# Value products with the values stationary, and three attention groups mixed feature by feature

## The chip, the core and the metric

The kernel runs on one core of a Trainium2 chip. The metric is device time in microseconds (us) of one execution. The kernel before took 1386.01 us, the median of three runs (1385.64, 1386.01 and 1386.95).

The engines are named as in the profile: PE multiplies matrices and writes PSUM, DVE and ACT do elementwise work, POOL does little here beside issuing transfers to its own software queue, and SP issues most transfers to a hardware queue. Each engine takes its instructions in program order, so an instruction that waits holds up everything behind it on that engine.

## The reference, cut to what matters

The program is one encoder layer for 1024 tokens of width 1024, all in float32. Its mixer A is a mixture of three dilated attention groups, four heads of 64 features each; the groups look at keys with a stride of 1, 4 and 16 tokens. For each token and head slot the three outputs are combined with weights that come from the softmax denominators:

```python
    s = jnp.einsum('brnqhd,brnkhd->brnhqk', qb, kw).astype(jnp.float32) * (dh ** -0.5) + bias
    s = jnp.where(mask[:, :, None], s, NEG_INF)
    m = jnp.max(s, axis=-1, keepdims=True)
    e = jnp.exp(s - m)
    den = jnp.sum(e, axis=-1, keepdims=True)
    o = jnp.einsum('brnhqk,brnkhd->brnhqd', e, vw) / den
    lse = (m + jnp.log(den))[..., 0]
...
        mix_w = jax.nn.softmax(jnp.stack(lses, axis=0), axis=0)
        y_attn = jnp.sum(mix_w[..., None] * jnp.stack(outs, axis=0), axis=0)
...
        merged = (jax.nn.sigmoid(gate_a) * (y_attn @ w_attn_branch[l])
                  + jax.nn.sigmoid(gate_g) * (y_gla @ w_gla_branch[l]))
```

The rest of the layer (the input projection, the gated linear attention, the output projection, two layer norms and the MLP) is left as it is by the change.

## The kernel before, in words

The large products are done by `mm3` (L97): each float32 operand is split into a high and a low part, and three matmuls (L101, L102, L103) take the place of one. Everything here concerns the stretch from about 300 us to 600 us, in which the input projection's remaining blocks run on PE and the attention is woven into them.

**Steps.** The projection blocks form a list `steps`; each step is one product of 12 matmuls over 512 columns with its evacuation from PSUM on DVE or ACT (L642 is the addition that evacuates most). A step's weights are prepared three steps ahead. The dictionary `units` hangs other work on a step's number: the attention's visits, and the gating of the other mixer.

**Visits.** `att(g, t)` makes the parts of one tile: group g, 128 queries t. There are 24 tiles, and `visit(i)` (L931) runs for neighbouring tiles, in this order, `load` of tile i+1 (POOL fetches queries and keys, L770), `values` of tile i-2, `scores` of tile i (POOL fetches the values, then PE computes the scores at L803, two heads at a time in the two halves of the array's rows, DVE adds the bias at L809 and ACT exponentiates at L814), `turned` of tile i-1 (PE transposes the exponentials at L830, and they are copied to `et`), then `mix` and `mixed`. The 27 visits are spread evenly over the steps. The tiles go by group: all eight of group 2, then of group 1, then of group 0.

**Value products** (L844). For each block of keys and each head, PE holds the transposed exponentials (keys x 128 queries) and streams the values (keys x 64 features) through; the result has a query per partition and 4 x 64 features in `avp`. Group 2 has one block of keys per tile, the other groups have two. A float32 product is two passes of the array, so the profile counts 320 matmuls for 160 products.

**Mixing.** Groups 2 and 1 write numerators and denominators of a tile as rows of 264 values to DRAM (`rows`, L857 and L859). A tile of group 0 reads the two other groups' rows back (L821), works out the weights (`weigh`, L878 to L884), multiplies and adds on DVE (`blend`, L887 to L898), transposes the result back to features on PE (L872), and writes it to `yadr` (L874): once per tile, eight times in all.

**Handing over.** After the attention, `branches` reads `yadr` back with SP (L963, tile `pre`), and ACT and DVE split it into high and low parts (`ya`, L148 and L149): four pieces, two feature halves by two halves of the tokens. `merge_a` (L1020) multiplies them by the branch weights, `merge_g` does the same for the other mixer's `yg`. That is the next work PE has after the last step.

**What sets the order.** The program is recorded in the order of the code, and a scheduler then orders each engine's instructions by its own time model. What is fixed is the data's dependences and the buffers.

Of the kernel before, what the change touches and what calls it, by code (L numbers as in the profile page):

```python
# [7 lines left out]
F32 = mybir.dt.float32  # L8
# [3 lines left out]
AF = mybir.ActivationFunctionType  # L12
# [5 lines left out]
S = 1024  # L18
# [53 lines left out]
def build(tc, io):  # L72
# [40 lines left out]
    rows = dr.tile([2, S, 264], F32, name="rows")  # L113
# [463 lines left out]
    px = cx.tile([128, 2, 512], F32R, name="px")  # L577
    wt = [[wp.tile([128, 2, 512], d, tag=t, bufs=n, name="p" + t) for _ in range(n)]
# [168 lines left out]
    sm_t, f_t = ring(ap_, [128, 8], F32, 3, "sm"), ring(ap_, [128, 5, 4], F32, 2, "f")  # L747
    st_t, R_t = ring(ap_, [128, 264], F32, 2, "st"), ring(ap_, [128, 3, 264], F32, 2, "R")
# [3 lines left out]
    yat = ap_.tile([128, 2, 128], F32, name="yat")  # L752
# [9 lines left out]
    def att(g, t):  # L762
# [54 lines left out]
        def turned():  # L817
            if g == 0:
                b["R"] = R_t()
                for i in range(2):  # L820
                    G.dma_start(b["R"][:, 1 + i], rows[i, t * 128:t * 128 + 128])  # L821
# [17 lines left out]
        def values():  # L839
            nb = len(b["blks"])  # L840

            def part(j, h):
                lo, hi, vv, p0 = b["blks"][j]
                return T.matmul(av[:, h * 64:h * 64 + 64], b["et"][h % 2][p0:p0 + vv.shape[0], h // 2, j],  # L844
                                vv[:, h * 64:h * 64 + 64], start=j == h == 0, stop=j == nb - 1,
                                skip_group_check=True)
# [6 lines left out]
            st = b["R"][:, 0] if g == 0 else st_t()  # L853
            V.tensor_copy(st[:, 0:256], av)
            V.tensor_copy(st[:, 256:264], b["sm"])
            if g == 1:
                G.dma_start(rows[0].rearrange("(u j c) w -> c u j w", u=2, c=4)[t // 2, t % 2], st)  # L857
            elif g == 2:
                G.dma_start(rows[1].rearrange("(j r) w -> r j w", r=8)[t], st)  # L859
            else:  # L860
                b["f"] = weigh(b["R"])

        def mix():
            if g == 0:
                b["o"] = o = st_t()[:, 0:256]
                blend(b["R"], b["f"], o)

        def mixed():
            if g == 0:
                tp = tr_t()  # L870
                for pr in range(2):
                    T.transpose(tp[:, pr, 0:128], b["o"][:, pr * 128:pr * 128 + 128], ident)  # L872
# [931 lines left out]
```

## Time and profile before

| what | us |
|---|---|
| median of three runs | 1386.01 |
| span of the profiled execution | 1382.5 |
| PE busy in it | 1373.9 (99%) |
| DVE busy | 1010.4 (73%) |
| ACT busy | 630.6 (46%) |
| POOL busy | 99.3 (7%) |

The page gives no time for the profiled execution other than its span, 1382.5 us from the first to the last instruction; the three runs are timed around the whole execution, and their median is 3.5 us longer. A change in the span is therefore carried over to the median as it is.

A row of the trace that begins with two numbers gives the start in us from the span's start and the length in us, then the engine, the line, the operation, the tiles (written <- read), the array's rows*columns in use, the shape and the count. A row with slashes gives the shortest, median and longest duration of a group in ns.

### The profile page before, as it was taken

To read this page: it belongs to the slowest core of one execution; us is meant where nothing else is said; L and a number is where in the kernel's file an instruction comes from. 1 tells how busy PE (TensorE), PEld (TensorE's weight loads), DVE (VectorE), ACT (ScalarE), POOL (GpSimd) and SP (SyncE) were. 2 spreads that over 40 slices of the span, in tenths; PEclk is the share of its full clock that TensorE was granted. 3 is DMA by queue.
4 is the path that set the end of the run, shared out by engine and by line. 5 is a ranking of instruction groups with operands and counts; after the bars stand their busy time and mean duration, and the time that the engine had idled before them with its cause. 6 is when DMAs were issued, how large, how long until landed. Compare 5 with 4: busy or idle time off the path is not lost.

```text
span 1382.5 us, 19028 instructions
## 1 busy us (share of the span) xinstructions
PE 1373.9 (99%) x6837; PEld 1152.6 (83%) x6837; DVE 1010.4 (73%) x1748; ACT 630.6 (46%) x1207; POOL 99.3 (7%) x153
## 2 busy tenths in 40 slices
PE   9999999999999999999999999999999999999998
PEld 7989998888888888888888788888888888888886
DVE  6377768776665678567757777877767897786988
ACT  5356645334434344455316655555456433333333
POOL 0000100022322232000001000000000000000002
PEclk9999999999999999999999999999999999999999
DMA  7262326765554443465934465656654965445313
GB/s 256 62 204 74 120 72 219 205 198 156 172 163 136 133 148 125 153 226 190 342 121 177 168 233 191 215 204 213 224 200 150 373 210 167 152 130 161 105 31 122
DMA packets 105907, 238.57 MB, mean 173 GB/s; under 512 B 20101, under 2 KB 28805, under 8 KB 105812
## 3 DMA queue, kind: packets, MB, share of 16 engines
q1 hardware_dynamic: 99220, 218.47, 47.4%
q0 software_dynamic: 6304, 18.49, 4.4%
q8 instruction: 54, 0.88, 0.3%
q10 hardware_dynamic: 288, 0.39, 0.1%
q14 instruction: 41, 0.34, 0.1%
HBM read 160.67 MB, written 77.68 MB: 172 GB/s over the span
## 4 chain that ended last, share of the span: by engine, by line
PE 96%; DVE 2%; ACT 1%; issue 0%; DMA 0%; SPq 0%; ACTq 0%; DVEq 0%
PE ps L101 18%; PE ps L103 18%; PE ps L102 18%; PE mm L101 10%; PE mm L102 10%; PE mm L103 10%; PE avp L844 3%; PE sc L803 2%; PE tr L830 2%; PE ps L1192 0%; PE sc L406 0%; PE tr L376 0%; DVE L L341 0%; PE sc L101 0%; PE sc L103 0%; PE sc L102 0%
## 5 line engine op out<-in xcount | busy, mean ns | idle before, releaser
L1176 ACT CAST T<-hp 128x1024 fp32r<-128x1024 f32 x36 | 37.8, 1050 | 110.3 <-PE ps L102 70.6
L102 PE MATMUL mm<-wlo,x 128*128 128x272 f32 (+1 forms) x240 | 74.5, 310 | 0.7 <-DVE wlo L94 0.7
L101 PE MATMUL mm<-whi,x 128*128 128x272 f32 (+1 forms) x240 | 75.0, 313 | 0.0
L103 PE MATMUL mm<-whi,x 128*128 128x272 f32 (+1 forms) x240 | 74.7, 311 | 0.0
L814 ACT ACTIVATE e<-e,sm 128x256 f32<-128x256 f32 (+2 forms) x96 | 43.4, 453 | 51.7 <-DVE sm L809 51.7
L102 PE MATMUL ps<-B,B 128*128 128x512 f32 x160 | 62.4, 390 | 0.0
L103 PE MATMUL ps<-B,B 128*128 128x512 f32 x160 | 62.3, 389 | 0.0
L101 PE MATMUL ps<-B,B 128*128 128x512 f32 x160 | 61.0, 391 | 0.5 <-ACT B L1176 0.5
L103 PE MATMUL ps<-B,T 128*128 128x512 f32 x144 | 56.2, 390 | 0.0
L101 PE MATMUL ps<-B,T 128*128 128x512 f32 x144 | 56.2, 390 | 0.0
L103 PE MATMUL ps<-T,T 128*128 128x512 f32 x144 | 56.1, 390 | 0.0
L101 PE MATMUL ps<-T,T 128*128 128x512 f32 x144 | 56.0, 389 | 0.0
L102 PE MATMUL ps<-T,T 128*128 128x512 f32 x144 | 56.0, 389 | 0.0
L102 PE MATMUL ps<-B,T 128*128 128x512 f32 x144 | 56.0, 389 | 0.0
L1177 DVE TENSOR_TENSOR T<-hp,T 128x1024 fp32r<-128x1024 f32 x36 | 43.9, 1220 | 15.3 <-ACT T L1176 15.2
L1577 DVE TENSOR_TENSOR acc<-ps,acc 128x512 f32<-128x512 f32 x68 | 45.5, 684 | 12.9 <-PE ps L103 12.2
L642 DVE TENSOR_TENSOR cr<-cu,mm 128x512 f32<-128x512 f32 x44 | 35.1, 799 | 23.7 <-PE mm L103 23.5
L1682 POOL TENSOR_TENSOR mv<-mv,mhalf 128x1 f32<-128x1 f32 x8 | 7.1, 882 | 611.4 <-DVE mv L1681 609.9
L101 PE MATMUL mm<-x,pwlo 128*128 128x512 f32 x128 | 51.0, 398 | 0.0
L101 PE MATMUL ps<-T,fraw 128*128 128x512 f32 x128 | 50.0, 394 | 0.3 <-ACT T L1176 0.3
L102 PE MATMUL ps<-T,fraw 128*128 128x512 f32 x128 | 50.1, 392 | 0.0
L103 PE MATMUL ps<-T,fraw 128*128 128x512 f32 x128 | 50.1, 392 | 0.0
(497 smaller groups left out, 4227.3 us busy)
## 6 DMA issues: line engine op xcount, KB each, us to landing
hdr<-c SPq DMA_DIRECT2D x112, 256.0 KB, 2.3
hp<-hdr SPq DMA_DIRECT2D x56, 512.0 KB, 3.6
spill<-cr SPq DMA_DIRECT2D x64, 256.0 KB, 2.8
praw<-in_wfm SPq DMA_DIRECT2D x16, 512.0 KB, 5.0
pwhi<-in_wfm SPq DMA_DIRECT2D x16, 512.0 KB, 4.5
gate<-spill SPq DMA_DIRECT2D x32, 256.0 KB, 3.4
wa<-in_w SPq DMA_DIRECT2D x16, 512.0 KB, 4.7
wb<-in_w SPq DMA_DIRECT2D x16, 512.0 KB, 6.3
```

Of the source, the lines that this page charges most:

```text
L101: T.matmul(ps, lh, rh, start=first and i == 0, stop=False, skip_group_check=more)
L102: T.matmul(ps, lh, rl, start=False, stop=False, skip_group_check=more)
L103: issued["pe"] = T.matmul(ps, ll, rh, start=False, stop=last and i == n - 1, skip_group_check=more)
L642: issued["add"] = V.tensor_tensor(o, a, b, op=OP.add)
L803: mm = T.matmul(sps[i][:, pr, 0:w], q[ps_, pr], k[ps_, pr, 0:w], start=True, stop=True)
L814: issued["exp"] = A.activation(e, e, AF.Exp, bias=sm[:, h:h + 1], scale=-1.0, accum_out=sm[:, 4 + h:5 + h])
L830: T.transpose(tp[0:hi - lo, pr, j], b["e"][i][:, pr, lo:hi], ident)
L844: return T.matmul(av[:, h * 64:h * 64 + 64], b["et"][h % 2][p0:p0 + vv.shape[0], h // 2, j], vv[:, h * 64:h * 64 + 64], start=j == h == 0, ...
L1176: A.copy(o[:, 0], src)
L1177: V.tensor_tensor(o[:, 1], src, o[:, 0].bitcast(F32), op=OP.subtract)
L1577: V.tensor_tensor(m, p, m, op=OP.add)
L1682: G.tensor_tensor(mv[:, 3:4], mv[:, 2:3], mhalf[:, 0:1], op=OP.pow)
```

## The change

Three things are done at once.

1. *Value products.* The values are now the operand that PE holds (keys x 64 features) and the transposed exponentials are streamed through (128 queries). Heads 0 and 2 go to the first 64 columns of the array and heads 1 and 3 to the last 64, so the result `avp` has a feature per partition and a query per column.
2. *Mixing.* All three groups write numerators, feature by feature, to `numdr`, and the maxima and denominators to `smdr`. For each 256 tokens (four times, `mixing(n)`, each in eight pieces hung on eight successive steps) the small values are fetched, the weights are worked out on DVE and ACT, transposed on PE (12 rows) and written to `fdr`. Then, for each half of the features, POOL reads back the numerators of the three groups (`mn`, two buffers) and, spread over 64 partitions, the weights (`mw`, three buffers); DVE multiplies and adds, and POOL writes the half to `yadr`. The transposes of the mixed result are gone.
3. *Order.* Tiles of group 1 and group 0 alternate by halves of the sequence, four and four, so that the first 256 tokens can be mixed at visit 15. There are 26 visits, spread up to three steps before the place where they ended. The pieces of `ya` are read last, after all of `yg`, and by halves of the tokens.

```diff
+    mn_t, mw_t = ring(cx, [128, 256], F32, 2, "mn"), ring(cx, [128, 256], F32, 3, "mw")
...
-    av = avp.tile([128, 256], F32, tag="av", name="avp")
+    av = avp.tile([128, 2, 128], F32, tag="av", name="avp")
...
             def part(j, h):
+                i, pr = h % 2, h // 2
                 lo, hi, vv, p0 = b["blks"][j]
-                return T.matmul(av[:, h * 64:h * 64 + 64], b["et"][h % 2][p0:p0 + vv.shape[0], h // 2, j],
-                                vv[:, h * 64:h * 64 + 64], start=j == h == 0, stop=j == nb - 1,
+                return T.matmul(av[64 * i:64 * i + 64, pr], vv[:, h * 64:h * 64 + 64],
+                                b["et"][i][p0:p0 + vv.shape[0], pr, j], start=j == pr == 0, stop=j == nb - 1,
                                 skip_group_check=True)
...
+            st = st_t()
+            V.tensor_copy(st, av)
+            G.dma_start(numdr[g, :, :, t * 128:t * 128 + 128].rearrange("b p n -> p b n"), st)
...
+            G.dma_start(own, b["sm"])
...
+    def mixing(n):
...
+        def spread():
+            tp = tr_t()[:, :, 0:128]
+            for t in range(2):
+                T.transpose(tp[0:12, t], m["f"][:, t, 0:3].rearrange("p g h -> p (g h)"), ident)
+            fT = mn_t()[0:12].rearrange("p (t n) -> p t n", t=2)
+            V.tensor_copy(fT, tp[0:12])
+            G.dma_start(fdr[:, sl].rearrange("p (t n) -> p t n", t=2), fT)
+
+        def load(pr, *gs):
+            for g in gs:
+                a, w = m[pr, g] = mn_t(), mw_t()
+                src = numdr[g, pr]
+                if g == 0:
+                    G.dma_start(a, src[:, sl])
+                else:
...
+                    for p in range(0, 128, 128 // g):
+                        ps_ = slice(p, p + 128 // g)
+                        G.dma_start(dst[ps_], src[ps_])
+                for i in range(2):
+                    row = fdr[4 * g + 2 * pr + i:4 * g + 2 * pr + i + 1, sl]
+                    G.dma_start(w[64 * i:64 * i + 64], row.to_broadcast([64, 256]))
+
+        def mix(pr, *gs):
+            o = m[pr, 0][1]
+            for g in gs:
...
+                V.tensor_tensor(wn, a.rearrange("p (c j) -> p j c", c=c), wn, op=OP.mult)
+                if g:
+                    V.tensor_tensor(o, o, w, op=OP.add)
+            if 2 in gs:
+                G.dma_start(yadr[pr, :, sl], o)
+
+        return [fetched, weigh, spread, lambda: load(0, 0, 1), lambda: (mix(0, 0, 1), load(0, 2)),
+                lambda: (mix(0, 2), load(1, 0, 1)), lambda: (mix(1, 0, 1), load(1, 2)), lambda: mix(1, 2)]
...
-    tiles = [att(g, t) for g in (2, 1, 0) for t in range(8)]
+    tiles = [att(2, t) for t in range(8)]
+    for u in range(2):
+        tiles += [att(1, 2 * c + u) for c in range(4)] + [att(0, 4 * u + c) for c in range(4)]
...
-    for i in range(27):
-        units.setdefault(n0 + 1 + i * (n1 - n0) // 27, []).append(lambda i=i: visit(i))
+    for i in range(26):
+        n = n0 + 1 + i * (n1 - 3 - n0) // 26
+        units.setdefault(n, []).append(lambda i=i: visit(i))
+        if i in (15, 17, 23, 25):
+            for j, f in enumerate(mixing((15, 17, 23, 25).index(i))):
+                units.setdefault(n + 1 + j, []).append(f)
...
-        for h in (0, 1):
+        for h in range(4):
             fed.extend(piece(yg[h // 2][:, :, h % 2, hf * 512:hf * 512 + 512], ygdr[h], hf) for hf in range(2))
-        for pr in range(2):
-            fed.extend(piece(ya[pr][hf], yadr[pr], hf) for hf in range(2))
...
+        for hf in range(2):
+            fed.extend(piece(ya[pr][hf], yadr[pr], hf) for pr in range(2))
```

How the engines' orders stand now, at three places. First PE, at the first value products (`avp`; `av` the values, `et` the transposed exponentials, `sc` the next tile's scores). Before:

```order
L103 MATMUL mm_2123<-x10_91,pwlo_2118 128x512
L844 MATMUL avp_2274<-av0_2251,et0_2258 128x64
L844 MATMUL avp_2274<-av0_2251,et1_2259 128x64
L844 MATMUL avp_2274<-av0_2251,et0_2258 128x64
L844 MATMUL avp_2274<-av0_2251,et1_2259 128x64
L803 MATMUL sc_2270<-ak0_2249,aq2_2248 128x128
```

The same place now:

```order
L103 MATMUL mm_2134<-x10_93,pwlo_2129 128x512
L844 MATMUL avp_2281<-et0_2269,av0_2262 64x128
L844 MATMUL avp_2281<-et1_2270,av0_2262 64x128
L844 MATMUL avp_2281<-et0_2269,av0_2262 64x128
L844 MATMUL avp_2281<-et1_2270,av0_2262 64x128
L806 MATMUL sc_2277<-ak0_2260,aq2_2259 128x128
```

Four products stand in the same place; their output is 64 partitions by 128 columns where it was 128 by 64, and neighbours alternate between the column halves.

Second DVE, behind the last step's evacuation (now at L646). Before, the four splits of `ya` (L149) stood among the last evacuations, the last of them ahead of the last three:

```order
L149 TENSOR_TENSOR ya00_4961<-pre_5028,ya00_4961 128x512
L149 TENSOR_TENSOR ya01_4962<-pre_5032,ya01_4962 128x512
L94 TENSOR_TENSOR wlo_5084<-raw_5080,whi_5082 128x768
L642 TENSOR_TENSOR cr1_2106<-cu1_2104,mm_2123 128x512
L149 TENSOR_TENSOR ya10_4963<-pre_5058,ya10_4963 128x512
L149 TENSOR_TENSOR ya11_4964<-pre_5062,ya11_4964 128x512
L642 TENSOR_TENSOR cr1_2106<-cr1_2106,mm_2124 128x512
```

Now nine multiplications and additions of the last 256 tokens (L920, L922) and two of the splits (L151) come behind the last evacuation:

```order
L646 TENSOR_TENSOR cr3_2110<-cu1_2106,mm_2135 128x512
L920 TENSOR_TENSOR mw0_2116<-mn0_2114,mw0_2116 128x256
L922 TENSOR_TENSOR mw0_2116<-mw0_2116,mw1_2117 128x256
L920 TENSOR_TENSOR mw2_2118<-mn0_2114,mw2_2118 128x256
L922 TENSOR_TENSOR mw0_2116<-mw0_2116,mw2_2118 128x256
L920 TENSOR_TENSOR mw1_2117<-mn0_2114,mw1_2117 128x256
L151 TENSOR_TENSOR ya01_4990<-pre_5155,ya01_4990 128x512
L920 TENSOR_TENSOR mw0_2116<-mn1_2115,mw0_2116 128x256
L922 TENSOR_TENSOR mw0_2116<-mw0_2116,mw1_2117 128x256
L920 TENSOR_TENSOR mw2_2118<-mn1_2115,mw2_2118 128x256
L922 TENSOR_TENSOR mw0_2116<-mw0_2116,mw2_2118 128x256
L151 TENSOR_TENSOR ya11_4992<-pre_5159,ya11_4992 128x512
```

The split of `ya01` (first feature half, last 512 tokens) stands ahead of the second feature half's mixing, and `ya11` at the very end.

Third PE, where the branches begin. Between the last projection matmul and the first row below stand 41 matmuls of 512 columns on `ya00`, `ya10` and `yg`:

```order
L103 MATMUL ps1_5187<-ya10_4991,wlo_5289 128x512
L101 MATMUL ps4_5190<-ya01_4990,whi_5101 128x512
L101 MATMUL ps6_5192<-ya01_4990,whi_5129 128x512
L101 MATMUL ps2_5188<-ya01_4990,whi_5287 128x512
L102 MATMUL ps4_5190<-ya01_4990,whi_5101 128x512
L103 MATMUL ps4_5190<-ya01_4990,wlo_5103 128x512
L102 MATMUL ps6_5192<-ya01_4990,whi_5129 128x512
L103 MATMUL ps6_5192<-ya01_4990,wlo_5131 128x512
L102 MATMUL ps2_5188<-ya01_4990,whi_5287 128x512
L103 MATMUL ps2_5188<-ya01_4990,wlo_5289 128x512
L101 MATMUL ps4_5190<-ya11_4992,whi_5101 128x512
L101 MATMUL ps6_5192<-ya11_4992,whi_5129 128x512
```

Before, `ya01` was multiplied from the seventh matmul behind the last projection on; now it comes after 42, and `ya11` nine later. POOL's own list has 226 transfers where it had 114.

More of the change, by code (lines that the diff above doesn't have):

```diff
@@ L112, in build @@
     yadr = dr.tile([2, 128, S], F32, name="yadr")
-    rows = dr.tile([2, S, 264], F32, name="rows")
+    numdr = dr.tile([3, 2, 128, S], F32, name="numdr")
+    smdr = dr.tile([3, S, 8], F32, name="smdr")
+    fdr = dr.tile([12, S], F32, name="fdr")
     tdr = dr.tile([12, 128, 512], F32, name="tdr")
@@ L817, in turned @@
         def turned():
[L818 to L821, printed above, removed]
             b["et"] = []
@@ L904, in build @@
     gated = ap_.tile([128, 3, 512], F32, tag="strip1", name="gated")
-    gating = (turns([flat(e_t()) for _ in range(4)] + [flat(R_t()) for _ in range(2)], 6),
+    gate_t = ap_.tile([128, 2, 512], F32, tag="strip0", name="gate_t")
+    gating = (turns([flat(e_t()) for _ in range(4)] + [gate_t[:, i] for i in range(2)], 6),
               turns([flat(et_t()) for _ in range(3)] + [gated[:, i] for i in range(3)], 6),
```

81 lines of the change are left out of this document (34 added, 47 removed).

## The prediction

> **What bounds the kernel now.** I read the busy times and the chain of waits first, then that chain's sum by line.
>
> ```profile
> PE 1373.9 (99%) x6837; PEld 1152.6 (83%) x6837; DVE 1010.4 (73%) x1748; ACT 630.6 (46%) x1207; POOL 99.3 (7%) x153
> PE 96%; DVE 2%; ACT 1%; issue 0%; DMA 0%; SPq 0%; ACTq 0%; DVEq 0%
> by line: PE ps L101 18.4%; PE ps L103 18.4%; PE ps L102 18.3%; PE mm L101 10.2%; PE mm L102 10.1%; PE mm L103 10.1%; PE avp L844 2.5%; PE sc L803 1.5%; PE tr L830 1.5%; PE ps L1192 0.4%; PE sc L406 0.4%; PE tr L376 0.4%; DVE L L341 0.3%; PE
> ```
>
> PE is the bound, and it has next to no idle time: what PE saves is saved from the time, and a wait that reaches PE is lost whole. The value products (L844) are 2.5% of 1382.5 us, 34.6 us, the scores (L803) and the turning of the exponentials (L830) 20.7 us each. The stretch of the change, by windows (us, then busy PE, PEld, DVE, ACT, POOL, clock, DMA share, GB/s), with the window at the very end below it:
>
> ```profile
> 300.00:594.00 294.00, 294.00 (x1628) 245.97 (x1628) 196.93 (x559) 124.23 (x348) 70.07 (x107) 1.00 0.47 151
> 1370.00:1382.40 12.40, 7.15 (x22) 3.50 (x20) 7.70 (x16) 2.42 (x7) 1.54 (x2) 0.88 0.35 128
> ```
>
> PE is busy for all 294 us at full clock; DVE and POOL have room there. So three things decide: the price of a value product, what PE waits for inside the stretch, and what it waits for where the attention hands over to the branches.
>
> **A. Value products.** The sizes, from the chain and the timeline of PE:
>
> ```profile
> L844 PE MATMUL avp<-av,et x320: 217/275/323, 314.7 to 562.9; 128*128 128x64 f32 x136, 64*128 64x64 f32 x24
> 314.82 0.84 PE avp L844 x8
> 398.06 1.73 PE avp L844 x16
> 302.93 0.65 PE sc L803 x8
> 399.80 1.06 PE sc L803 x8
> 468.90 1.13 PE L803 MATMUL sc<-ak,aq 64*128 64x256 f32 x8
> 469.97 1.06 PE L830 MATMUL tr<-ident,e 128*64 128x128 f32 x8
> 470.79 0.48 PE L101 MATMUL mm<-x,pwlo 128*128 128x512 f32 x1
> ```
>
> A tile with one block of keys takes 0.84 us (8 passes), one with two blocks 1.73 (16); 8 × 0.84 + 16 × 1.73 = 34.4, the chain's 34.6. Of the new form (64 result columns of the array, 128 columns streamed) no row exists. If the two halves of the array's columns work at once, the nearest is the scores: two heads in the two halves of the rows, 8 passes, 0.65 us with 128 keys per head and 1.06 with 256. A one-block tile then costs 0.65, a two-block tile, which streams as much as the longer scores, 1.06: 8 × 0.65 + 16 × 1.06 = 22.2, **−12.4 us**, which I take. Bounds: without what it costs to begin a small product, (1.06 − 0.65) = 0.41 per block, 40 blocks 16.4, −18. If the halves run one behind the other, the nearest is the turning in the half-column mode: eight passes from 469.97 to 470.79, 0.82 us, 40 blocks 32.8, and 0.24 per tile for beginning (0.65 − 0.41) makes 38.6, +4.
>
> The Trainium skill ("TensorE: Matmul & The Clock Gate", The mechanism) says that a weight load runs beside a matmul only where their row groups differ, and two column halves share their rows; by it A would be nearer +4 than −12. Against it stand the eight turnings above, which share rows too.
>
> ```profile
> L830 PEld LDWEIGHTS tr<-ident,e x160: 108/140/198, 309.1 to 553.5; 128*128 128x128 f32 x140, 128*64 128x64 f32 x20
> ```
>
> Each took 0.82/8 = 0.10 us with loads of 0.11 to 0.20 of their own, so loads there were hidden; whether products of two halves are, no row shows.
>
> **B. Transposes on PE, and what costs nothing.** 16 rows (L872) go, 8 of the weights come, at 1.06/8 = 0.13: **−1.0**. The tiles' new order changes no count of products, loads or evacuations; the two buffers that the gating no longer borrows from the mixing are replaced one for one. The mixing's 24 products and 16 sums on DVE stand for 24 and 16 of the same size, hidden under PE as before (DVE has 294 − 197 = 97 us free in the stretch), apart from where they wait (D, E).
>
> **C. Waiting inside the stretch.** A mixing's transposes stand on PE between the attention's, in the same `tr` buffers, and need the small values: a write, a fetch, and a few DVE operations of 0.15 us (below, L890). Writing and fetching are 3.0 + 2.6 us by the rows below, some 8 us with the operations and exponentials; a step between two visits' parts is 12 matmuls of 0.227 us (the 21 from 459.32 to 464.09), 2.7 us, and fetch, weights and transposes hang on three successive steps, 8.2 us. So it about fits, and a tile that writes late makes PE wait the difference, with the projection queued behind. Nothing to 2 us in each of the three mixings inside the stretch, 0 to 6: I take **+2.5**.
>
> ```profile
> 459.32 0.40 PE L103 MATMUL mm<-xT,pwlo 128*128 128x512 f32 x1
> ...
> 464.09 0.39 PE L103 MATMUL mm<-xT,pwlo 128*128 128x512 f32 x1
> rows<-st POOLq DMA_DIRECT2D x16, 132.0 KB, 3.0
> R<-rows POOLq DMA_DIRECT2D x16, 132.0 KB, 2.6
> yadr<-yat POOLq DMA_DIRECT2D x8, 128.0 KB, 2.9
> pre<-yadr SPq DMA_DIRECT2D x4, 256.0 KB, 3.0
> L821 POOL DMA_DIRECT2D R<-rows x16: 539/554/569, 377.4 to 545.5; - x16
> L874 POOL DMA_DIRECT2D yadr<-yat x8: 713/724/747, 502.7 to 570.8; - x8
> L890 DVE TENSOR_TENSOR f<-R x8: 154/156/164, 468.0 to 550.1; 128x4 f32<-128x4 f32 x8
> L896 DVE TENSOR_TENSOR R<-R,f x24: 413/419/427, 468.8 to 563.6; 128x256 f32<-128x256 f32 x24
> L897 DVE TENSOR_TENSOR R<-R x8: 415/422/425, 483.6 to 564.1; 128x256 f32<-128x256 f32 x8
> L148 ACT CAST ya<-pre x4: 619/623/624, 583.1 to 588.3; 128x512 fp32r<-128x512 f32 x4
> L149 DVE TENSOR_TENSOR ya<-pre,ya x4: 686/689/689, 586.9 to 590.2; 128x512 fp32r<-128x512 f32 x4
> L642 DVE TENSOR_TENSOR cr<-cu,mm x44: 679/687/1143, 243.2 to 597.0; 128x512 f32<-128x512 f32 x44
> ```
>
> POOL's transfers go from 114 to 226 (40 removed, 152 added). At 0.55 to 0.72 us of issue each that is 84 to 109 us more than the 22 to 29 that go; with the 70 busy now it fits into 294.
>
> **D. The hand-over.** Before, `ya` was ready by 590.2 and PE did not wait. Now the last 256 tokens are mixed at the very end. Take T as the end of the last projection matmul. By the order, the last weights' trip through DRAM is then about to land; I take 2 us more. Then, in a chain in which each waits for the one before:
>
> - first feature half: product and sum 0.42 + 0.42 = 0.8 (L896, L897); fetch of group 2, which must wait for buffers (two of `mn`, three of `mw`) to come free: two issues of weights, spread over 64 partitions each. Their price no row has; I estimate 0.7 each from L821 and L874 and 2.6 to land, 4.0; product and sum 0.8; `yadr` written 2.9 and its issue 0.6, 3.5; read by SP 3.0; split 0.62 + 0.69 = 1.3. `ya01` is there at T + 2 + 0.8 + 4.0 + 0.8 + 3.5 + 3.0 + 1.3 = T + 15.4.
> - second half: its fetch waits for the first half's buffers and its last product on DVE stands behind `ya01`'s split, which waits for the read: 0.8 + 4.0 + 0.8 + 3.0 + 3.0 + 1.3 = 12.9 more, T + 28.3.
>
> PE's cover is 42 matmuls on `ya00`, `ya10` and `yg`, and nine on `ya01`: 51 × 0.227 = 11.6 us. The wait is 28.3 − 11.6 = **+16.7**, about 6 of it at `ya01` and 11 at `ya11`. Bounds: if the weights land by T and both halves' fetches run side by side, 5 to 6 us go, +11; if each trip takes the slowest that its tiles show, 5.7 us where 3.0 is taken, it is two trips × 2.7 more, +22.
>
> ```profile
> DMA to landing us min/median/max: 2.8/3.0/5.7
> DMA to landing us min/median/max: 2.2/3.0/5.7
> ```
>
> (the first for `pre`, the second for `yadr`).
>
> **E. DVE's queue.** A product or sum that waits for its fetch holds back the projection's evacuations behind it (L642, 0.69 us each), and with them PSUM. Behind them PE cannot begin a new block for want of a PSUM buffer. By one to three evacuations in the last steps, 0.5 to 2, **+1.5**.
>
> **F. Clock.** Behind the idle gaps at the end of the program the granted clock is 0.88: 12% × 12.4 us is 1.5 us. Two long waits in D make such a stretch: **+1.5** (0 to 3). The Trainium skill ("TensorE: Matmul & The Clock Gate", Part 1) has the clock halve after an idle window of some 3.4 us and come back after as long a busy one; by it F would be up to 1.7 for each wait, which is inside those ends.
>
> **Sum.** −12.4 − 1.0 + 2.5 + 16.7 + 1.5 + 1.5 = +8.8 on the span of 1382.5; the median is 3.5 above the span, so 1386.0 + 8.8 = **1395**. With A's and D's ends moderate (A −14 to −9, D 12 to 20) the case spans 1387 to 1404.
>
> **Rivals.**
>
> - *The column halves do not overlap.* A becomes +4, 16 us worse. For it: two products of one key block share the array's rows, and the scores that serve as price use different rows. Against it: the turnings' 0.10 us. The hand-over gets no shorter by it, since the last tile is later too: 1394.8 + 16.4 = 1411.
> - *Overlap at the floor, a short hand-over.* A −18 with no cost of beginning, D at +12.5, C 0.5, E and F 1 together: −18 − 1 + 12.5 + 0.5 + 1 = −5: 1381. For it: PE does pay 0.41 per further block in the scores, and the halves have buffers enough to overlap partly. Against it: every other small product here pays its beginning. With these prices the change gains as long as D stays under 17.5 us; with mine, under 7.9.
> - *POOL's queue.* POOL issues in order: a spread fetch that waits for a free buffer or for `fdr` holds back the next tile's queries, keys and values, and PE's scores wait. Four such fetches (one in each mixing) at 2.6 us add 10: 1405. For it: 152 added issues, with the waiting ones in the middle. Against it: 24 tiles between 314.7 and 562.9 us (L844) are 10 us apart, and a tile's queries and keys are asked for a visit early.
> - *It does nothing of the kind to the end:* PE's order has `ya` last, but if the scheduler's order held the mixing well ahead (the last `yadr` before T), D would vanish, with F: 1386 − 12.4 − 1.0 + 2.5 + 1.5, 1377. The order speaks against it: nine products and sums stand behind the last evacuation.
>
> **How the numbers follow.** Forecast 0.55; no overlap 0.15; overlap at the floor 0.18; POOL's queue 0.10; the last 0.02. A change under 0.2%, 2.8 us, cannot be told from none here. Faster: four fifths of the second rival and the last, 0.17; within 0.2%: what is left of the second, and 0.07 of the forecast with A and D at their good ends, 0.11; slower 0.72. The range 1380 to 1412 leaves out the faster part of the second rival (0.07), the last (0.02) and the slower half of the first (0.07 to 0.08).
>
> **What would show it.** Right: the two-block tiles of the value products near 1.06 us in the chain and L844's share near 1.6%; a wait of PE at `ya01` and a longer one at `ya11` just behind the projection, whose chain runs through `yadr`, `pre` and group 2's fetch; a granted clock under 1 there. Wrong: value products at 1.7 us or more (first rival), no PE idle time over 5 us at the branches (second), or waits of PE at the scores for queries or keys (third). D is the term that would overthrow the forecast most: if the fetches of the second half run beside those of the first, half of its 17 us go.

## The result, and the profile after

The changed kernel takes 1421.74 us, the median of four runs (1420.2 to 1424.2), 1.0257 times the kernel before, with an interval of 1.0245 to 1.027. The forecast was 1395 and a range of 1380 to 1412: right in sign, too small by a factor of four in size. The profiled execution has a span of 1417.6 us, 35.1 longer than before.

The page's busy times and PE's waits (engine and line that waited, what for: total us, times, longest) of the changed kernel:

```profile
PE 1376.5 (97%) x6829; PEld 1136.2 (80%) x6829; DVE 1007.0 (71%) x1696; ACT 627.0 (44%) x1195; POOL 169.2 (12%) x265
PE ps L101 <- ACT ya L150: 14.9, 2, 9.9
PE mm L101 <- DVE cr L646: 11.9, 2, 9.3
PE tr L829 <- DVE mn L894: 2.8, 1, 2.8
PE avp L844 <- DVE et L836: 2.6, 1, 2.6
```

Before, PE's longest wait was 1.2 us, at the very start, and between 300 and 660 us none is listed; now six waits there come to 32.2 us. DVE has no more work than before; it is late, not full. The first row is the hand-over of term D, the third is term C. The second is term E: PE cannot begin a projection block because an evacuation (L646) has not run. I had 1.5 us for it. The fourth is of the same kind as the second. PE waits there, from 513 to 516 us, for a copy of the exponentials (`et`), and DVE comes to that copy late because it had stood before two products of the mixing, 4.3 us for numerators (the first row) and another 1.3 for weights:

```profile
507.94 0.63 DVE L920 TENSOR_TENSOR mw<-mn,mw 128x256 f32<-128x256 f32 x1 [4.33 <-DMA mn<-numdr]
...
515.40 0.68 DVE L836 COPY et<-tr 128x512 f32<-128x512 f32 x1
```

**Value products.** PE's timeline of the changed kernel, around a tile with one block of keys and one with two; below it the same two places before:

```profile
315.72 0.39 PE L103 MATMUL mm<-x,pwlo 128*128 128x512 f32 x1
316.04 0.66 PE L844 MATMUL avp<-et,av 128*64 128x128 f32 x8
316.62 0.71 PE L806 MATMUL sc<-ak,aq 64*128 64x128 f32 x8
...
396.55 0.39 PE L103 MATMUL mm<-xT,pwhi 128*128 128x512 f32 x1
396.87 1.24 PE L844 MATMUL avp<-et,av 128*64 128x128 f32 x16
398.04 0.92 PE L806 MATMUL sc<-ak,aq 64*128 64x192 f32 x8
```

```profile
314.43 0.39 PE L103 MATMUL mm<-x,pwlo 128*128 128x512 f32 x1
314.66 1.00 PE L844 MATMUL avp<-av,et 128*128 128x64 f32 x8
315.58 0.71 PE L803 MATMUL sc<-ak,aq 64*128 64x128 f32 x8
...
397.68 0.39 PE L103 MATMUL mm<-xT,pwhi 128*128 128x512 f32 x1
397.90 1.89 PE L844 MATMUL avp<-av,et 128*128 128x64 f32 x16
399.73 1.13 PE L803 MATMUL sc<-ak,aq 64*128 64x256 f32 x8
```

Read from the start of the matmul ahead to the start of the one behind, less 0.23 for the matmul itself. The one-block tile costs 0.67 us where it was 0.92; the two-block tile 1.26 where it was 1.82. That is 8 × 0.25 + 16 × 0.56 = 11.0 us less, in tiles that run in one piece. Where a projection matmul stands between a tile's products some of it is lost, since entering the new form now costs 0.32 instead of 0.23 (315.72 to 316.04) and leaving it 0.2.

**Where PE stops in the projection.** DVE, PE and POOL of the changed kernel around the longest wait there (start, length, engine, line, what; in brackets the idle time before and what ended it), and PE's clock in that window (0.51, third number from the end):

```profile
596.26 0.95 DVE L94 TENSOR_TENSOR wlo<-raw,whi 128x768 fp32r<-128x768 f32 x1
604.06 0.59 DVE L920 TENSOR_TENSOR mw<-mn,mw 128x256 f32<-128x256 f32 x1 [6.85 <-issue]
604.57 0.68 DVE L646 TENSOR_TENSOR cr<-cu,mm 128x512 f32<-128x512 f32 x1
```

```profile
595.59 0.39 PE L103 MATMUL mm<-xT,pwhi 128*128 128x512 f32 x1
605.30 0.80 PE L101 MATMUL mm<-xT,pwlo 128*128 128x512 f32 x1 [9.32 <-DVE cr L646]
...
610.48 0.39 PE L101 MATMUL mm<-x,px 128*128 128x512 f32 x1
```

```profile
598.14 0.72 POOL L909 DMA_DIRECT2D mn<-numdr  x1 [4.05 <-DVE wlo L94]
601.41 0.69 POOL L909 DMA_DIRECT2D mn<-numdr  x1 [2.54 <-issue]
...
614.96 0.71 POOL L909 DMA_DIRECT2D mn<-numdr  x1 [3.95 <-DVE mw L922]
```

```profile
600.00:610.00 10.00, 4.70 (x11) 3.73 (x12) 5.05 (x9) 0.12 (x1) 4.54 (x9) 0.51 0.26 82
```

A product of the mixing (L920) stands on DVE ahead of an evacuation that PE needs. Its numerators come from group 2's two sorted fetches (L909, 512 pieces each, at 598.14 and 601.41), and ahead of the second POOL stands for 2.5 us, having waited for nothing that the trace names. So DVE stands for 6.9 us, PE for 9.3, and then PE runs twelve matmuls at half its clock (605.30 to 610.48 is 5.2 us where twelve take 2.7).

The source row of L909 in the changed kernel (what ended POOL's idle time ahead of it: us, times; and issue to landing of the tile) shows how often:

```profile
  issue: 31.2, 12
DMA to landing us min/median/max: 2.4/2.7/6.2
```

Twelve of the 24 fetches wait 31.2 us, from 0.35 to 5.9 us each. The second of group 2's two fetches is among them in all eight pairs, with 2.0 us or more each time and 24.0 in all; the median from issue to landing is 2.7. Ahead of its other transfers POOL stands for another 30.3 us without a named reason, where the kernel before has 0.5 in all between 300 and 660 us. 12.5 of the 30.3 are ahead of the tiles' queries, keys and values, and PE never waits for one of these.

### The profile page after: what moved, and what is told of

Same layout as the page of the kernel before. It is cut to its first block, busy times and chain, and to the rows that moved or that the text cites. A ratio compares the mean times of both kernels' runs of the same rounds, so it can differ in the third digit from the quotient of the medians.

```text
span 1417.6 us, 19178 instructions
## 1 busy us (share of the span) xinstructions
PE 1376.5 (97%) x6829; PEld 1136.2 (80%) x6829; DVE 1007.0 (71%) x1696; ACT 627.0 (44%) x1195; POOL 169.2 (12%) x265
## 4 chain that ended last, share of the span: by engine, by line
PE 54%; DMA 1%; issue 1%; DVE 1%; ACT 1%; POOL 0%; DVEq 0%; POOLq 0%; ACTq 0%
PE ps L101 18%; PE ps L103 18%; PE ps L102 18%; DMA mn<-numdr 1%; PE ps L1226 0%; DMA pre<-yadr 0%; DMA yadr<-mw 0%; PE mm L101 0%; ACT xr L1229 0%; PE mm L102 0%; PE mm L103 0%; DVE acc L1719 0%; ACT T L1210 0%; DVE acc L1723 0%; DVE mw L920 0%
## 5 line engine op out<-in xcount | busy, mean ns | idle before, releaser
L101 PE MATMUL mm<-xT,pwlo 128*128 128x512 f32 x112 | 46.7, 417 | 9.3 <-DVE cr L646 9.3
L1211 DVE TENSOR_TENSOR T<-hp,T 128x1024 fp32r<-128x1024 f32 x36 | 44.0, 1223 | 14.9 <-ACT T L1210 14.8
L920 DVE TENSOR_TENSOR mw<-mn,mw 128x256 f32<-128x256 f32 x24 | 13.2, 550 | 56.5 <-DMA mn<-numdr 28.3
L646 DVE TENSOR_TENSOR cr<-cu,mm 128x512 f32<-128x512 f32 x44 | 35.1, 798 | 23.9 <-PE mm L103 23.8
L101 PE MATMUL mm<-x,pwlo 128*128 128x512 f32 x128 | 51.0, 399 | 0.0
L103 PE MATMUL mm<-x,pwlo 128*128 128x512 f32 x128 | 50.4, 393 | 0.0
```

The lines of the kernel that those rows point to most:

```text
L101: T.matmul(ps, lh, rh, start=first and i == 0, stop=False, skip_group_check=more)
L103: issued["pe"] = T.matmul(ps, ll, rh, start=False, stop=last and i == n - 1, skip_group_check=more)
L646: issued["add"] = V.tensor_tensor(o, a, b, op=OP.add)
L920: V.tensor_tensor(wn, a.rearrange("p (c j) -> p j c", c=c), wn, op=OP.mult)
L1211: V.tensor_tensor(o[:, 1], src, o[:, 0].bitcast(F32), op=OP.subtract)
```

## The experiments

The theories. **Q**: POOL's queue does not take two 512-piece fetches at once, and this lateness, passed on by DVE's order, makes E and some of D. **B**: too few buffers, and too many trips in a row, whatever the pieces. Two further questions: whether it is really the evacuations behind waiting products that stop PE, and whether the column halves run at once.

**Fetches without sorting.** Group 2's numerators in one transfer of 128 pieces, group 1's in one of 256. The sorting into token order is left out.

```diff
-                    src = src.rearrange("p (c u q j) -> p u q c j", c=c, u=2, q=2)[:, u, q]
-                    dst = a.rearrange("p (c j) -> p c j", c=c)
-                    for p in range(0, 128, 128 // g):
-                        ps_ = slice(p, p + 128 // g)
-                        G.dma_start(dst[ps_], src[ps_])
+                    if g == 2:
+                        G.dma_start(a, src[:, sl])
+                    else:
+                        src = src.rearrange("p (c u j) -> p u c j", c=c, u=2)[:, u, 0:2]
+                        G.dma_start(a.rearrange("p (c j) -> p c j", c=2), src)
```

> The changed kernel, with the sorting into token order left out: group 2's numerators are fetched in one transfer of 128 pieces (not two of 512), group 1's in one of 256 (not 512), so columns are mixed in the wrong order; buffers, weights and arithmetic stay. Theory Q (POOL's queue does not carry two 512-piece fetches at once; the second is issued only when the first has landed, and that lateness holds DVE's products and the evacuations behind them): the 31.2 us in which POOL stands before L909 for no shown reason fall under 8, PE's waits on evacuations fall from 11.9 to under 4, those on ya from 14.9 to 8 to 11, time 1398 to 1408. Rival B (the buffers and the number of trips in the chain are what is late, whatever the pieces): the waits stay within 20%, time 1416 or more.

1397.3 us (1394.8 to 1399.9), against 1385.9 for the kernel before and just under what was expected. PE's waits:

```profile
PE ps L101 <- ACT ya L150: 9.8, 2, 8.4
PE tr L829 <- DVE mn L894: 3.3, 1, 3.3
```

The waits on evacuations are gone altogether, and POOL's unexplained idle time ahead of L909 is 0.2 us. 24.4 of the 35 us go with the sorting. Q holds, B doesn't.

**A buffer of its own for the transposed weights.**

```diff
-            fT = mn_t()[0:12].rearrange("p (t n) -> p t n", t=2)
+            fT = ft_t()[0:12].rearrange("p (t n) -> p t n", t=2)
```

> The changed kernel, but the transposed weights (fT) get a buffer of their own instead of one of the two for numerators. Theory B (that buffer is held until the weights' write has landed, and the numerators' fetches behind it start too late): PE's waits on evacuations fall from 11.9 to 5 or less, time 1410 to 1415. Theory Q (512-piece fetches one at a time): at most one trip of the four mixings is earlier, waits on evacuations 9 or more, time 1418 to 1422.

1420.3 us (1419.8 to 1420.9). The waits on evacuations are 10.7 us in three pieces; no more than 1.4 us is gained. B is out as the main cause.

**Sorted fetches on SP's queue.** The same pieces, the same buffers, another queue.

```diff
-                        G.dma_start(dst[ps_], src[ps_])
+                        SP.dma_start(dst[ps_], src[ps_])
```

> The changed kernel, with the sorted fetches of groups 1 and 2 issued by SP to its hardware queue instead of POOL's. Theory Q (the limit is POOL's queue): the second of two fetches follows the first at once; PE's waits on evacuations under 5 and on ya 8 to 11, time 1400 to 1410, unless SP's own work (weights, spills) waits behind them, which would show as waits of the projection for weights. Rival B (buffers and trips): 1416 or more.

1394.6 us (1392.8 to 1395.9), even less than I expected. PE's two longest waits:

```profile
PE ps L101 <- ACT ya L150: 8.6, 1, 8.6
PE tr L829 <- DVE mn L894: 3.9, 1, 3.9
```

The sorting into 512 pieces costs next to nothing in itself (1397.3 us without it); on POOL's queue it costs 27 us. That the kernel now stands at the forecast's 1395 is luck: the hand-over waits 8.6 us where 16.7 were forecast, the value products gain less, and half clock behind the two waits takes about 5 where 1.5 was taken. POOL's waits without a named reason are not all gone either. Between 300 and 660 us they fall from 61.5 us to 31.2, now all ahead of other transfers; what makes these is not shown.

**Products and sums on POOL.**

```diff
-                V.tensor_tensor(wn, a.rearrange("p (c j) -> p j c", c=c), wn, op=OP.mult)
+                G.tensor_tensor(wn, a.rearrange("p (c j) -> p j c", c=c), wn, op=OP.mult)
...
-                    V.tensor_tensor(o, o, w, op=OP.add)
+                    G.tensor_tensor(o, o, w, op=OP.add)
```

> The changed kernel, with the mixing's products and sums (L920, L922) on POOL instead of DVE, so that no evacuation of the projection stands behind a product that waits for its fetch. Theory E (the evacuations behind waiting products are what stops PE inside the projection): waits on evacuations go from 11.9 to under 1 and the slow clock behind them, 4 us, goes too; the waits on ya become 0 to 8 longer (POOL's products are slower and hold its transfers back); time 1404 to 1414. If the projection stops for another reason: waits of 9 or more stay and the time is 1420 or more.

1431.9 us (1430.8 to 1432.9), a miss in the time. In the waits it is a hit: those on DVE's evacuations are gone from the list, so waiting products were what held them. But POOL now alternates products and transfers, and the hand-over's wait more than doubles:

```profile
PE ps L101 <- ACT ya L150: 34.6, 2, 23.9
...
PE mm L101 <- ACT cr L671: 1.0, 1, 1.0
```

**Fetches of 256 pieces on POOL.**

```diff
-                    for p in range(0, 128, 128 // g):
-                        ps_ = slice(p, p + 128 // g)
+                    for p in range(0, 128, 64 // g):
+                        ps_ = slice(p, p + 64 // g)
```

> The changed kernel, with each sorted fetch on POOL cut into two with half the partitions: 256 pieces each instead of 512, 48 transfers instead of 24. Theory Q1 (POOL's queue holds a limited number of outstanding pieces, more than some 830 and less than 1024 plus): the second and third of a row of fetches follow at once after 0.6 us, and only from about the fourth on POOL waits for a landing; the 31.2 us of waiting without a shown reason fall by a third to two thirds, time 1405 to 1418. Rival Q2 (one sorted fetch at a time, whatever its size): 24 more waits of 2 us or more, time 1430 or more.

1414.9 us (1414.4 to 1415.5). POOL's timeline and L909's row:

```profile
610.14 1.82 POOL L909 DMA_DIRECT2D mn<-numdr  x3 [2.99 <-DVE mw L922]
612.51 0.58 POOL L909 DMA_DIRECT2D mn<-numdr  x1 [0.56 <-issue]
```

```profile
  issue: 13.2, 12
```

Three follow each other at once, the fourth waits until 2.4 us after the first was issued, about when that one lands (the median from issue to landing is 2.4). So it is neither one sorted fetch at a time nor the making of each piece; it fits a limit on what is outstanding, 768 pieces being taken and 1024 not (Q1). The idle time falls from 31.2 to 13.2 us.

PE's waits on evacuations fall to 1.3 us, but those on `ya` rise to 31.1. PE's timeline shows why, from the first matmul of the branches on:

```profile
590.26 0.39 PE L101 MATMUL ps<-ya,whi 128*128 128x512 f32 x1
...
623.24 1.65 PE L101 MATMUL ps<-ya,whi 128*128 128x512 f32 x3 [22.48 <-ACT ya L150]
...
636.04 1.65 PE L101 MATMUL ps<-ya,whi 128*128 128x512 f32 x3 [8.59 <-ACT ya L150]
```

The projection is through at 590.3 us, 23 us before the changed kernel's 613.2, and PE then stands at the branches for the mixing, whose last split of `ya` ends at 636.7 where it ended at 642.2. The run with products on POOL looks alike (594.4, and 651.9 for the split). So the waits inside the projection and those at the branches are one lateness, paid at two places: what sets the time is when the mixing's chain ends. From that last split to the end of the span the changed kernel takes 775.4 us and the five runs so far 775 to 778.

**Neighbours in the same column half.**

```diff
-                    for h in range(4):
+                    for h in (0, 2, 1, 3):
```

> The changed kernel, with the four products of a block in the order of heads 0, 2, 1, 3, so that neighbours lie in the same column half. Theory (the two halves work at once, which is why a pass of L844 starts 0.065 us behind the one before, against 0.109 before the change): pairs in the same half go at about 0.11, the mean between passes rises to 0.085 to 0.11, which is 285 x 0.02 to 0.045 = 6 to 13 us more work on PE, partly taken from the waits behind it: time 1424 to 1434. Rival (a 64-column product is simply shorter, and no two run at once): the mean stays 0.065 and the time 1420 to 1423.

1422.1 us (1422.0 to 1422.2), and a one-block tile takes nearly the same, 0.59 us to the next row:

```profile
316.29 0.66 PE L844 MATMUL avp<-et,av 128*64 128x128 f32 x8
316.88 0.71 PE L806 MATMUL sc<-ak,aq 64*128 64x128 f32 x8
```

The number is that of the rival, that a 64-column product is simply shorter. The next run on this question shows that its reason is wrong. No row of the trace tells which head a product belongs to, so that the neighbours on PE did lie in the same half is not shown.

**All four heads in one column half**, on the quickest kernel by then (the 1383.3 below).

```diff
-    av = avp.tile([128, 2, 128], F32, tag="av", name="avp")
+    av = avp.tile([128, 4, 128], F32, tag="av", name="avp")
...
-                return T.matmul(av[64 * i:64 * i + 64, pr], vv[:, h * 64:h * 64 + 64],
-                                b["et"][i][p0:p0 + vv.shape[0], pr, j], start=j == pr == 0, stop=j == nb - 1,
+                return T.matmul(av[0:64, h], vv[:, h * 64:h * 64 + 64],
+                                b["et"][i][p0:p0 + vv.shape[0], pr, j], start=j == h == 0, stop=j == nb - 1,
...
-            V.tensor_copy(st, av)
+            for i in range(2):
+                V.tensor_copy(st[64 * i:64 * i + 64], av[0:64, i:4:2])
```

> The kernel at 1383.3 (SP's fetches, the direct split, later mixings, three numerator buffers), with all four heads' products in the first column half of the array; two copies with 64 partitions each take the place of one behind them on DVE. Theory (the halves run at once): a pass follows the one before by about 0.11 us instead of 0.064, 287 x 0.046 = 13 us more: 1394 to 1398. Rival (a 64-column product is quick by itself): 1383 to 1386.

```profile
315.55 1.09 PE L844 MATMUL avp<-et,av 128*64 128x128 f32 x8
316.57 0.71 PE L806 MATMUL sc<-ak,aq 64*128 64x128 f32 x8
...
400.29 2.10 PE L844 MATMUL avp<-et,av 128*64 128x128 f32 x16
402.32 0.92 PE L806 MATMUL sc<-ak,aq 64*128 64x192 f32 x8
```

A one-block tile now takes 1.02 us to the next row where it took 0.58, a two-block tile 2.03 where it took 1.17. So the halves do run at once. The single starts say the same: in the changed kernel the first tile's passes start in pairs, 7 ns apart, with 0.11 to 0.16 us from pair to pair, and here they start singly, with the same distance from pass to pass. Why changing the order of heads in the code (the run before) made no difference stays open. The time is 1392.5 (1392.5 to 1394.3), 9 us more and not 13. The likely reason is that the attention lasts longer and the fetches have more time: no wait over 1.0 us is left beside the 1.2 at the start.

**The hand-over's trip.** On the kernel with SP's fetches, the last 256 tokens are split into `ya` from the mixing's buffer, without `yadr`; the read-back of the last 512 tokens then covers their first 256 only.

```diff
-            if 2 in gs:
+            if 2 in gs and n == 3:
+                halve(ya[pr][1][:, 0, 256:512], ya[pr][1][:, 1, 256:512], o)
+            elif 2 in gs:
                 G.dma_start(yadr[pr, :, sl], o)
```

> The kernel with SP's sorted fetches (1394.6) with one more edit: the last 256 tokens are split into ya straight from the mixing's buffer, not written to yadr and read back. If the trip through yadr is what the hand-over waits for: the wait on ya falls from 8.6 to 3 or less and the slow clock behind it goes, time 1384 to 1388; the 3.9 before the transposes stay. If the fetches of the second half are the later ones: the wait stays at 5 or more, time 1390 or more.

1389.5 us (1388.6 to 1391.6), 5 less than 1394.6; the wait on `ya` falls from 8.6 to 4.6. Between the two cases: the trip is about half of it, and what the rest is this run does not show.

**With the first two mixings later as well** (weights, transposes and what follows by one to two steps), and then **with three numerator buffers**.

```diff
-                units.setdefault(n + 1 + j, []).append(f)
+                units.setdefault(n + 1 + j + (min(j, 2) if i < 20 else 0), []).append(f)
...
-    mn_t, mw_t = ring(cx, [128, 256], F32, 2, "mn"), ring(cx, [128, 256], F32, 3, "mw")
+    mn_t, mw_t = ring(cx, [128, 256], F32, 3, "mn"), ring(cx, [128, 256], F32, 3, "mw")
```

> The kernel with SP's sorted fetches (1394.6), and two more edits: the last 256 tokens are split into ya straight from the mixing's buffer, without the trip through yadr; and in the first two mixings the weights, the transposes and all that follows come one to two steps later. If the hand-over's trip and the first mixing's transposes are what is left: the wait on ya falls from 8.6 to 2 or less, the 3.9 before the transposes goes, with 2 to 3 us of slow clock: 1380 to 1385. If the fetches behind reused buffers are the limit instead: the wait on ya stays at 5 or more, 1387 to 1391.

> As the run before it, with three buffers for numerators instead of two. If reused buffers still delay the second feature half's fetches at the end: 1 to 4 us less than the run before. If only the trip and the transposes counted: within 1 us of it.

1386.9 (1384.4 to 1390.6; ratio 0.9993 to 1.0014), which misses both of the times that I gave first: the waits on `ya` and on the transposes went, but evacuations behind the mixing took 6.2 us in three waits. With the third buffer 1383.3 (1380.7 to 1384.1; 0.9949 to 0.9977): 3.6 us from one buffer, and 0.2 to 0.5% less than the kernel before.

**Steps and queue of the small values.** First the first mixing three steps later and the third two; then the maxima and denominators fetched by SP too.

```diff
-(min(j, 2) if i < 20 else 0)
+(min(j, 1) * 3 if i < 16 else min(j, 2) if i < 24 else 0)
...
-                G.dma_start(sm[:, :, g], smdr[g, sl].rearrange("(t p) w -> p t w", p=128))
+                SP.dma_start(sm[:, :, g], smdr[g, sl].rearrange("(t p) w -> p t w", p=128))
```

> The kernel at 1383.3, with the first mixing's weights and all behind them three steps later than recorded at first (two before) and the third mixing's two steps later. If the 3.6 us of waits at the first mixing come from weights that DVE begins before the maxima and denominators have landed: they go, 1379 to 1381. If the late tile is late whatever the place: within 1 us of 1383.3.

> As the run before it, with the maxima and denominators fetched by SP's queue instead of POOL's, where they stand behind the tiles' own loads. If POOL's order makes them late: 1 to 3 us less. If SP's own order does the same to them: within 1 us, or longer.

1392.4 (1388.2 to 1394.6), a clear miss: a third mixing that comes later pushes the fourth, and PE waits 8.0 us on `ya`. The wait at the first mixing stays (2.3), so the place was not its cause. With SP's small fetches 1387.1 (1384.0 to 1391.8), 5 us less where I expected 1 to 3: the first mixing's wait is gone, the 7.8 on `ya` stay.

**Both, with the third mixing back in its place; and the 1383.3 kernel with SP's small fetches alone.**

```diff
-(min(j, 1) * 3 if i < 16 else min(j, 2) if i < 24 else 0)
+(min(j, 1) * 3 if i < 16 else min(j, 2) if i < 20 else 0)
```

> SP's sorted fetches, the direct split of the last 256 tokens, three numerator buffers, maxima and denominators fetched by SP, first two mixings three and two steps later, third mixing where it stood at first. If the value products' own gain is the 8 us that their passes show, and only the named waits hid it (7.8 at ya, with some 1 of slow clock, in the run at 1387.1): 1377 to 1380. If waits come back at another place: 1382 or more.

> The kernel at 1383.3 with the maxima and denominators fetched by SP, and nothing else changed. If POOL's order made them late: the waits at the first mixing (2.8 and 0.8) go and the others (1.8 and 2.1) stay, 1379 to 1381. If the number of steps is what counts: within 1 us of 1383.3.

1382.6 (1380.2 to 1385.8; ratio 0.9965 to 0.9982) and 1382.7 (1380.7 to 1383.9; 0.9963 to 0.9984): the two are equal, and as quick as the 1383.3 within what the runs tell apart. Both miss the shorter times that I gave (1377 to 1380 and 1379 to 1381). In the first the waits that I had named went, and 2.5 us came back at `ya`; in the second the first mixing's waits fell to 0.7, and the time is still within 1 us of 1383.3. The waits of the first of them:

```profile
PE ps L101 <- ACT ya L150: 2.5, 1, 2.5
...
PE mm L101 <- DVE cr L646: 0.5, 1, 0.5
```

Its span is 1379.7, 2.8 under the kernel before, with 3.0 us of waits in it. So the value products and the transposes that went (terms A and B) are worth more than 5.8 us there; about 1 to 1.5 of half clock behind the 2.5 us wait, as behind the one of the same length in the changed kernel below, and 1.6 by which it is later than before ahead of any changed work (the matmul ahead of its first value product starts at 315.99, before at 314.43) make it 8 to 9.

## Why the prediction was wrong

**The step that failed is E**, "DVE's queue": "By one to three evacuations in the last steps, 0.5 to 2". The mechanism was the right one (a waiting product holds back evacuations, and PE runs out of PSUM); the size was not. It measured 11.9 us of waits on evacuations and 2.6 on the copy of `et`, with 4.0 of half clock behind the former. I asked how many evacuations stand behind a product, and not how long the product waits. That length came from a price that no row of before could show. For group 2's fetch the forecast had "4.0": two issues of 0.7, one right behind the other, and 2.6 to land. On POOL's queue the second is held back for 2.0 us or more in all eight pairs; 614.96 to DVE's product at 620.31 is 5.4. In the hand-over this is 1.4 us per half; inside the projection it comes back in each half of each mixing, the chain falls behind the steps on which it hangs, and the lateness arrives at DVE.

With it fails the premise on which D starts, that the last weights are "about to land" when the projection ends. The run with fetches of 256 pieces shows it: there the projection is not held up, T is 590.3, and `ya01` comes at T + 33.6 where D had T + 15.4. By these rows, taking E's waits away alone would have gained little; the chain itself had to become shorter, and on SP's queue it did.

**A and B, value products and transposes: −13.4 forecast, 8 to 9 gained.** That the halves run at once was right (1.09 against 0.66 us when they cannot). What was mis-sized is the two-block tile, 1.26 where the scores' row gave 1.06, and what is lost where a projection matmul stands between. The rule of the Trainium skill ("TensorE: Matmul & The Clock Gate", The mechanism), that a weight load runs beside a matmul only where their row groups differ, had led me to +4 as the other end; the measured 1.09 against 0.66 decides against what I drew from it. B, −1.0, is too small to be read apart.

**C, waits inside the stretch: +2.5 forecast, 2.8 measured**, at the first mixing's transposes. The runs with the small fetches on SP's queue show why: the first mixing's values were late through POOL's order.

**D, the hand-over: +16.7 forecast, 14.9 measured.** Counted from T, the end of the last projection matmul (613.2), the steps came out nearly as forecast. I had `ya01` at T + 15.4 = 628.6 and `ya11` at T + 28.3 = 641.5. DVE's timeline of the changed kernel, with the product that waits for the fetch and the two splits:

```profile
620.31 0.63 DVE L920 TENSOR_TENSOR mw<-mn,mw 128x256 f32<-128x256 f32 x1 [5.43 <-DMA mn<-numdr]
...
627.82 0.69 DVE L151 TENSOR_TENSOR ya<-pre,ya 128x512 fp32r<-128x512 f32 x1 [2.98 <-ACT ya L150]
...
641.48 0.69 DVE L151 TENSOR_TENSOR ya<-pre,ya 128x512 fp32r<-128x512 f32 x1 [5.80 <-ACT ya L150]
```

The splits end at 628.5 and 642.2. Two things of this are luck. The fetch was longer than priced (5.4) and the weights' 2 us were not needed, so the errors offset each other; and T had itself been put back by E's waits, which gave the late chain its time.

**F, clock: +1.5 forecast, about 8.6 measured.** Behind each wait the matmuls follow each other by 0.43 us instead of 0.23: seven matmuls or so behind the 2.5, 5.0 and 9.9 us waits and behind the 2.8 at the transposes (about 1.5 each), twelve behind the 9.3 (2.5). I had allowed for two waits and there were five. (Two slips in the working changed nothing: two waits at up to 1.7 us each, as stands beside F, would be 3.4, just over the end of 3; and A's and D's moderate ends add up to 1388.5 and 1401.5, not 1387 and 1404.)

**The sum.** 32.2 of waits + 8.6 of clock − 9 of value products + 1.3 by which the matmul ahead of the first value product was later (315.72 against 314.43) = 33 of the 35.1 us; 2 are not broken down.

**The rivals.** "POOL's queue" (0.10, 1405) named the queue, but had it hold back the tiles' loads, for 10 us of PE's time. POOL did stand 12.5 us ahead of these loads, but PE waited for none; it was the mixing's own fetches, for 24 to 27 us. The other three fall: the halves overlap, not at the floor, and the mixing does reach past T.

## What to carry to other kernels

When transfers of many small pieces are added to a queue, ask what the queue takes at once, not only what one of them costs; put them on the queue whose owner has time, here one line for 27 us. A product that waits for a transfer should not stand in the order of an engine that evacuates PSUM, unless its data are there well ahead; price it by how late the data can be. Waits in two places can be one lateness: follow the late chain to its end before adding them up as separate costs. And most waits of PE of 2.5 us or more were paid a second time in half clock here, so several short ones cost more than one of the same sum.

## What the runs showed of the hardware

- POOL's queue took 768 pieces (three sorted fetches of 256) at once, and held back the fetch that would have made 1024 until about when the first had landed (2.4 us). With fetches of 512 pieces the second of a pair was held back in all eight pairs, for 2.0 to 5.9 us; the trace gives no releaser. SP's queue took the same fetches without such a wait (two of them in 1.2 us, from 588.33).
- Two products that hold values in the two column halves, on the same rows, run at once: 0.58 us to the next row for eight passes, 1.02 us with all of them in one half.
- PE's clock fell to half behind a wait of 2.5 us already, for 3.1 us (583.34 to 586.48). Behind the wait of 9.3 us twelve matmuls took 5.2 us, but behind the one of 9.9 us the slow stretch was 3.1 again. One wait of 2.6 us left the clock at 1.00:

```profile
583.34 0.80 PE L101 MATMUL mm<-x,px 128*128 128x512 f32 x1 [2.53 <-DVE cr L646]
...
586.48 0.40 PE L102 MATMUL mm<-x,px 128*128 128x512 f32 x1
```

```profile
512.00:520.00 8.00, 5.38 (x41) 3.96 (x40) 5.23 (x16) 4.06 (x12) 6.66 (x12) 1.00 0.63 175
```

The trace's record of the granted clock explains the difference. Half clock is granted in the changed kernel from 460.15 to 463.56, 583.03 to 586.44, 600.10 to 610.34, 627.41 to 630.82 and 634.23 to 644.47: stretches of 3.41 us or three times that, whose starts lie whole multiples of 3.41 apart. So a long wait uses up part of its half clock while PE still stands. Laid on this grid, a stretch at full clock in which PE stood 2.1 us or more was followed by half clock in every run here, and one with 2.0 or less in none. The wait of 2.6 us lay across two stretches, about 1.4 us in each; of the 2.5 us ahead of 583.34 about 2.4 lay in one.

The Trainium skill ("TensorE: Matmul & The Clock Gate", Part 1) speaks of a window of about 3.4 us that runs freely, and of half clock after an idle one. Length and free running agree with the trace; that a window must be idle throughout does not, since 2.1 us were enough.
